# Clipping a gradient by its norm: larger transfers, another split of the work between two engines, and a smaller first store

## The chip, the cores and the metric

One core of a Trainium2 chip. The metric is device time in microseconds (us) of one execution. Some executions of a kernel come out some per cent longer than the others; a run more than 1.5% above the fastest of its kernel is called slow here. Every profiled execution in this study was in the fast state with a granted clock of 1.00; one timed run was slow (52.76 us, in e8), and verdicts use fast runs alone. A profiled execution has a span (here about 1.8 us shorter than the device time of the same execution, 49.9 against 51.7 for the kernel before), and all positions below are microseconds from the start of that span. Sixteen transfer (DMA) engines move the data. In the packet records here one row of a tile is one packet, the 128 rows of a transfer are shared among the sixteen engines, and each engine reports its part with one small completion packet.

## The reference

```python
batch, dim = 512, 4096                      # grad: 512 x 4096 float32, 8.4 MB
norm  = np.sqrt(np.sum(grad ** 2))
scale = min(1.0, max_norm / (norm + 1e-8))  # max_norm = 1.0
return (grad * scale).astype(np.float32)
```

Nothing can be stored before everything has been loaded, since the scale depends on all elements. The whole gradient fits into on-chip memory as four blocks of 128 rows, so it is read once and written once. With the input here the norm is over ten thousand, and the added 1e-8 is far below one unit in the last place.

## The kernel before

Loads of 2048 columns, each squared partly on ScalarE (ACT) and partly on VectorE (DVE); the last 2048 columns are loaded as 1536 and 512, and the 512 go to DVE alone.

```python
LOAD_COLS = 2048; TAIL_COLS = 512; ACT_SQ = 768; ST_COLS = 2048; ACT_MUL = 896
for b, c0, w in loads:
    nc.sync.dma_start(out=gt[b][:, c0:c0+w], in_=g[b*P:(b+1)*P, c0:c0+w])
    a_w = min(ACT_SQ, w // 2) if w > TAIL_COLS else 0
    if a_w:                                  # ACT: square, row sums into one column of acc
        nc.scalar.activation(out=sq, in_=gt[b][:, c0:c0+a_w], func=Square,
                             accum_out=acc[:, icol:icol+1]); icol += 1
    nc.vector.tensor_tensor_reduce(          # DVE: the other columns
        out=sqd, in0=gt[b][:, c0+a_w:c0+w], in1=gt[b][:, c0+a_w:c0+w],
        op0=mult, op1=add, accum_out=acc[:, icol:icol+1], ...); icol += 1

nc.vector.reduce_sum(out=s, in_=acc, axis=X)
nc.tensor.matmul(tot, ones, s, start=True, stop=True)     # sum over partitions
nc.scalar.activation(out=nrm, in_=tot, func=Sqrt, bias=0.0)
nc.vector.tensor_scalar(out=nrm2, in0=nrm, scalar1=1e-8, op0=add, ...)
nc.vector.reciprocal(out=inv, in_=nrm2)
nc.vector.tensor_scalar(out=scale, in0=inv, scalar1=max_norm, scalar2=1.0, op0=mult, op1=min)

for b in range(4):
    for c0 in (0, 2048):                     # DVE 1152 columns, ACT 896, then one store of both
        nc.vector.tensor_scalar(out=gt[b][:, c0:c0+1152], ..., scalar1=scale, op0=mult)
        nc.scalar.mul(gt[b][:, c0+1152:c0+2048], ..., scale)
        nc.sync.dma_start(out=o[...], in_=gt[b][:, c0:c0+2048])
# ... (pools, constants and the launch are cut)
```

Of the kernel before, what the change touches and what calls it, by code (L numbers as in the profile page):

```python
# [1 line left out]

# [4 lines left out]


@with_exitstack  # L10
def kernel(
    ctx: ExitStack,
    tc: tile.TileContext,
    grad: bass.AP,
    max_norm: bass.AP,
    out: bass.AP,
):
    nc = tc.nc
    fp32 = mybir.dt.float32
    bf16 = mybir.dt.bfloat16  # L20

    g = grad.flatten_outer_dims()
    o = out.flatten_outer_dims()
    R, C = g.shape
    P = nc.NUM_PARTITIONS
    assert R % P == 0, (R, P)
    nrow_blk = R // P

    LOAD_COLS = 2048
    TAIL_COLS = 512  # L30
    ACT_SQ = 768
    ST_COLS = 2048
    ACT_MUL = 896
    assert C % LOAD_COLS == 0 and C % ST_COLS == 0

    loads = []
    for b in range(nrow_blk):
        for j in range(C // LOAD_COLS):
            c0 = j * LOAD_COLS
            w = LOAD_COLS  # L40
            if b == nrow_blk - 1 and j == C // LOAD_COLS - 1 and TAIL_COLS:
                loads.append((b, c0, LOAD_COLS - TAIL_COLS))
                loads.append((b, c0 + LOAD_COLS - TAIL_COLS, TAIL_COLS))
            else:
                loads.append((b, c0, w))

    sbuf = ctx.enter_context(tc.tile_pool(name="gbuf", bufs=1))
    small = ctx.enter_context(tc.tile_pool(name="small", bufs=1))
    scratch = ctx.enter_context(tc.tile_pool(name="scratch", bufs=3))
    psum_pool = ctx.enter_context(tc.tile_pool(name="psum", bufs=2, space=bass.MemoryType.PSUM))  # L50

    gt = [sbuf.tile([P, C], fp32, name=f"g{b}", tag=f"g{b}") for b in range(nrow_blk)]

    n_acc = sum(2 if w > TAIL_COLS else 1 for _, _, w in loads)
    acc = small.tile([P, n_acc], fp32)
    ones = small.tile([P, P], fp32)
    zcol = small.tile([P, 1], fp32)
    dcol = small.tile([P, 1], fp32)
    nc.gpsimd.memset(ones, 1.0)  # L59
    nc.gpsimd.memset(zcol, 0.0)  # L60

    nc.scalar.activation(out=dcol, in_=zcol, func=mybir.ActivationFunctionType.Sqrt)  # L62

    icol = 0
    for b, c0, w in loads:
        nc.sync.dma_start(  # L66
            out=gt[b][:, c0 : c0 + w],
            in_=g[b * P : (b + 1) * P, c0 : c0 + w],
        )
        a_w = min(ACT_SQ, w // 2) if w > TAIL_COLS else 0  # L70
        if a_w:
            sq = scratch.tile([P, a_w], bf16, name="sqa", tag="sqa")
            nc.scalar.activation(  # L73
                out=sq,
                in_=gt[b][:, c0 : c0 + a_w],
                func=mybir.ActivationFunctionType.Square,
                accum_out=acc[:, icol : icol + 1],
            )
            icol += 1
        d_w = w - a_w  # L80
        sqd = scratch.tile([P, d_w], bf16, name="sqd", tag="sqd")
        nc.vector.tensor_tensor_reduce(  # L82
            out=sqd,
            in0=gt[b][:, c0 + a_w : c0 + w],
            in1=gt[b][:, c0 + a_w : c0 + w],
            scale=1.0,
            scalar=0.0,
            op0=mybir.AluOpType.mult,
            op1=mybir.AluOpType.add,
            accum_out=acc[:, icol : icol + 1],  # L90
        )
        icol += 1
    assert icol == n_acc

    s = small.tile([P, 1], fp32)
    nc.vector.reduce_sum(out=s, in_=acc, axis=mybir.AxisListType.X)  # L96

    tot = psum_pool.tile([P, 1], fp32, name="tot", tag="tot")
    nc.tensor.matmul(tot, ones, s, start=True, stop=True)  # L99

    nrm = small.tile([P, 1], fp32)
    nc.scalar.activation(  # L102
        out=nrm, in_=tot, func=mybir.ActivationFunctionType.Sqrt, bias=0.0
    )
    nrm2 = small.tile([P, 1], fp32)
    nc.vector.tensor_scalar(  # L106
        out=nrm2, in0=nrm, scalar1=1e-8, scalar2=None, op0=mybir.AluOpType.add
    )
    inv = small.tile([P, 1], fp32)
    nc.vector.reciprocal(out=inv, in_=nrm2)  # L110
    scale = small.tile([P, 1], fp32)
    nc.vector.tensor_scalar(  # L112
        out=scale,
        in0=inv,
        scalar1=float(max_norm),
        scalar2=1.0,
        op0=mybir.AluOpType.mult,
        op1=mybir.AluOpType.min,
    )

    for b in range(nrow_blk):
        for j in range(C // ST_COLS):
            c0 = j * ST_COLS
            dcols = ST_COLS - ACT_MUL
            nc.vector.tensor_scalar(  # L125
                out=gt[b][:, c0 : c0 + dcols],
                in0=gt[b][:, c0 : c0 + dcols],
                scalar1=scale[:, 0:1],
                scalar2=None,
                op0=mybir.AluOpType.mult,  # L130
            )
            nc.scalar.mul(  # L132
                gt[b][:, c0 + dcols : c0 + ST_COLS],
                gt[b][:, c0 + dcols : c0 + ST_COLS],
                scale[:, 0:1],
            )
            nc.sync.dma_start(
                out=o[b * P : (b + 1) * P, c0 : c0 + ST_COLS],
                in_=gt[b][:, c0 : c0 + ST_COLS],
            )  # L140


# [1 line left out]
_INS = ['grad', 'max_norm']  # L144
_OUTS = [((512, 4096), 'float32')]
#: Inputs that are plain numbers.
_NUMBERS = {'max_norm': 1.0}


# [26 lines left out]
```

## Time and profile before

| | before |
|---|---|
| time, median | 51.41 us in 3 runs at first; 51.44 us in the 15 runs beside the changed kernel |
| span of the profiled execution | 49.92 us |
| last-but-one load piece (1536 columns) landed | 22.97 |
| first store issued / its first packet | 27.55 / 28.40 |
| last packet of the last store ended / its completion landed | 48.57 / 48.93 |

Issues are read in the timeline, the first store's in this line (SPq is the queue of SyncE, which issues all transfers):

```profile
27.55 8.97 SPq L137 DMA_DIRECT2D out_dram<-g  x8
```

Packets and landings are in the trace's packet and semaphore records (a landing is the arrival of the last engine's completion signal, some tenths of a microsecond after the last packet). The views themselves are shown in the prediction. In short: load at full transfer rate, a gap with idle transfer engines, store at full rate.

### The profile page before, as it was taken

The page shows a single profiled execution, that of the slowest core. Times are in us where ns is not written, and L with a number is a line of the kernel's source. Part 1 is how long each engine was busy: PE and PEld are TensorE (multiplying, and loading weights), DVE is VectorE, ACT ScalarE, POOL GpSimd, SP SyncE. Part 2 cuts the span into 40 slices and gives each one's busy share as a digit, 9 for nine tenths or more (in the row PEclk, how much of TensorE's full clock was granted, in tenths as well). Part 3 has the DMA queues.
Part 4 walks back from the last instruction along what each step waited for, and adds up shares of the span by engine and source line. Part 5 has one row for each costly group of instructions (what it writes and reads, how often), then busy time and mean ns, then how long its engine had stood idle before and what let it go on. Part 6 is the DMA issues. An engine that isn't in the chain of part 4 may idle for free.

```text
span 49.9 us, 148 instructions
## 1 busy us (share of the span) xinstructions
PE 0.6 (1%) x2; PEld 0.5 (1%) x2; DVE 18.6 (37%) x30; ACT 16.7 (33%) x27; POOL 0.4 (1%) x6
## 2 busy tenths in 40 slices
PE   0000000000000000000040000000000000000000
PEld 0000000000000000000040000000000000000000
DVE  0000192929192929295929999900000000000000
ACT  4700161515161615155217999992000000000000
POOL 3000000000000000000000000000000000000000
DMA  0699999999999999980000299999999999999970
GB/s 0 118 302 420 427 427 420 427 433 420 433 433 427 420 420 415 402 345 33 0 0 0 105 420 420 420 420 420 420 420 420 420 420 420 420 420 420 420 315 0
DMA packets 2448, 16.78 MB, mean 336 GB/s; under 512 B 272, under 2 KB 272, under 8 KB 528
## 3 DMA queue, kind: packets, MB, share of 16 engines
q1 hardware_dynamic: 2448, 16.78, 82.0%
HBM read 8.39 MB, written 8.39 MB: 336 GB/s over the span
## 4 chain that ended last, share of the span: by engine, by line
DMA 37%; ACT 14%; SPq 7%; DVE 4%; issue 2%; ACTq 2%; PE 1%; DVEq 0%
DMA g<-in_grad_dram 37%; ACT g L132 13%; SPq L66 7%; DVE sqd L82 2%; ACTq L171 2%; PE tot L99 1%; DVE s L96 0%; ACT nrm L102 0%; DVE inv L110 0%; DVE nrm L106 0%; DVE scale L112 0%; DVE acc L82 0%; DVEq L96 0%; DVEq L82 0%
## 5 line engine op out<-in xcount | busy, mean ns | idle before, releaser
L82 DVE CUSTOM_DVE_ANT_0 sqd<-g 128x1280 bf16<-128x1280 f32 (+2 forms) x9 | 12.0, 1344 | 12.6 <-DMA g<-in_grad_dram 12.6
L73 ACT ACTIVATE sqa<-g 128x768 bf16<-128x768 f32 x8 | 6.7, 843 | 14.3 <-DMA g<-in_grad_dram 14.3
L132 ACT ACTIVATE g<-g,scale 128x896 f32<-128x896 f32 x8 | 7.6, 1028 | 0.6 <-DVE scale L112 0.6
L125 DVE TENSOR_SCALAR g<-g,scale 128x1152 f32<-128x1152 f32 x8 | 5.9, 815 | 0.0
L62 ACT ACT_TABLE_LOAD x1 | 1.3, 1283 | 0.7 <-PEq L157 0.7
L73 ACT ACTIVATION_READ_ACCUMULATOR sqa<-g 128x1 f32 x8 | 1.5, 187 | 0.0
L99 PE MATMUL tot<-s,ones 128*128 128x1 f32 x2 | 0.6, 348 | 25.1 <-DVE s L96 25.1
L99 PEld LDWEIGHTS tot<-s,ones 128*128 128x128 f32 x2 | 0.5, 313 | 25.1 <-issue 25.1
L82 DVE DVE_READ_ACCUMULATOR2_ANT acc<- 128x1 f32 x9 | 0.7, 83 | 0.0
L102 ACT ACTIVATE nrm<-tot 128x1 f32<-128x1 f32 x1 | 0.2, 171 | 1.7 <-PE tot L99 1.7
L106 DVE TENSOR_SCALAR nrm<-nrm 128x1 f32<-128x1 f32 x1 | 0.2, 155 | 0.9 <-ACT nrm L102 0.9
L96 DVE TENSOR_REDUCE s<-acc 128x1 f32<-128x17 f32 x1 | 0.2, 172 | 0.1
L59 POOL MEMSET ones<- 128x128 f32 x1 | 0.2, 205 | 0.3 <-POOLq L157 0.3
L62 ACT ACTIVATE dcol<-zcol 128x1 f32<-128x1 f32 x1 | 0.2, 203 | 0.0
L110 DVE RECIPROCAL inv<-nrm 128x1 f32<-128x1 f32 x1 | 0.2, 164 | 0.0
L112 DVE TENSOR_SCALAR scale<-inv 128x1 f32<-128x1 f32 x1 | 0.2, 154 | 0.0
L157 POOL MEMSET const-bfloat16-1.0<- 128x1 bf16 x1 | 0.1, 102 | 0.0
L157 POOL MEMSET const-uint8-127<- 128x1 uint8 x1 | 0.1, 102 | 0.0
L157 POOL MEMSET const-float32-0.0<- 128x1 f32 x1 | 0.1, 99 | 0.2 <-issue 0.2
L60 POOL MEMSET zcol<- 128x1 f32 x1 | 0.1, 99 | 0.0
L157 POOL MEMSET const-float32-1.0<- 128x1 f32 x1 | 0.1, 98 | 0.0
## 6 DMA issues: line engine op xcount, KB each, us to landing
out_dram<-g SPq DMA_DIRECT2D x8, 1024.0 KB, 9.3
g<-in_grad_dram SPq DMA_DIRECT2D x7, 1024.0 KB, 11.4
g<-in_grad_dram SPq DMA_DIRECT2D x1, 768.0 KB, 18.4
g<-in_grad_dram SPq DMA_DIRECT2D x1, 256.0 KB, 17.5
```

Source lines behind the costliest of these rows:

```text
L59: nc.gpsimd.memset(ones, 1.0)
L62: nc.scalar.activation(out=dcol, in_=zcol, func=mybir.ActivationFunctionType.Sqrt)
L66: nc.sync.dma_start(out=gt[b][:, c0 : c0 + w], in_=g[b * P : (b + 1) * P, c0 : c0 + w],)
L73: nc.scalar.activation(out=sq, in_=gt[b][:, c0 : c0 + a_w], func=mybir.ActivationFunctionType.Square, accum_out=acc[:, icol : icol + 1],)
L82: nc.vector.tensor_tensor_reduce(out=sqd, in0=gt[b][:, c0 + a_w : c0 + w], in1=gt[b][:, c0 + a_w : c0 + w], scale=1.0, scalar=0.0, op0=myb ...
L96: nc.vector.reduce_sum(out=s, in_=acc, axis=mybir.AxisListType.X)
L99: nc.tensor.matmul(tot, ones, s, start=True, stop=True)
L102: nc.scalar.activation(out=nrm, in_=tot, func=mybir.ActivationFunctionType.Sqrt, bias=0.0)
L125: nc.vector.tensor_scalar(out=gt[b][:, c0 : c0 + dcols], in0=gt[b][:, c0 : c0 + dcols], scalar1=scale[:, 0:1], scalar2=None, op0=mybir.Alu ...
L132: nc.scalar.mul(gt[b][:, c0 + dcols : c0 + ST_COLS], gt[b][:, c0 + dcols : c0 + ST_COLS], scale[:, 0:1],)
L157: nc = _bacc.Bacc("TRN2", target_bir_lowering=False, num_devices=1)
L171: with _tile.TileContext(nc) as tc:
```

## The change

The intent is to spend less on the transfers themselves (whole rows of 16 KB instead of halves of 8 KB), to shorten the serial part between load and store, and to start the store with a small piece. Which engine multiplies what is changed to match. The change also lowers two buffer counts (scratch 3 to 2, PSUM 2 to 1), which no run tests alone; e1 keeps the old counts and shows the same gap. Core of the diff, with cuts marked:

```diff
+    for b in range(nb - 1):
+        loads.append((b, 0, C, None))                 # three loads of 128 x 4096
+    loads.append((lb, 0, C - PRE - TAIL, None))       # 2048 columns
+    loads.append((lb, C - PRE - TAIL, PRE, "A"))      # 1536
+    loads.append((lb, C - TAIL, TAIL, "D"))           # 512, DVE alone
...
-        a_w = min(ACT_SQ, w // 2) if w > TAIL_COLS else 0
+            a_w = 1152 if eng == "A" else (w * 5 // 8) & ~7
...
-    nc.vector.tensor_scalar(
-        out=nrm2, in0=nrm, scalar1=1e-8, scalar2=None, op0=mybir.AluOpType.add
-    )
-    nc.vector.reciprocal(out=inv, in_=nrm2)
+    nc.vector.reciprocal(out=inv, in_=nrm)
...
-    (eight stores of 2048 columns, each DVE 1152 + ACT 896)
+    stores.append((0, 0, 512, [("D", 0, 512)]))
+    stores.append((0, 512, 1024, [("A", 512, 1024)]))
+    stores.append((0, 1536, C - 1536, [("D", 1536, C - 1536)]))
+    stores.append((1, 0, C, [("A", 0, C)]))
+    stores.append((2, 0, C, [("D", 0, C)]))
+    stores.append((3, 0, C, [("A", 0, C // 2), ("D", C // 2, C // 2)]))
```

More of the change, by code (lines that the diff above doesn't have):

```diff
@@ L7 @@
 from concourse._compat import with_exitstack
+CFG = dict(
+    TAIL_COLS=512,
+    PRE_TAIL=1536,
+    ST_FIRST=1024,
+)
 @with_exitstack
@@ L26 @@
     assert R % P == 0, (R, P)
-    nrow_blk = R // P
-    LOAD_COLS = 2048
-    TAIL_COLS = 512
-    ACT_SQ = 768
-    ST_COLS = 2048
-    ACT_MUL = 896
-    assert C % LOAD_COLS == 0 and C % ST_COLS == 0
-    loads = []
-    for b in range(nrow_blk):
-        for j in range(C // LOAD_COLS):
-            c0 = j * LOAD_COLS
-            w = LOAD_COLS
-            if b == nrow_blk - 1 and j == C // LOAD_COLS - 1 and TAIL_COLS:
-                loads.append((b, c0, LOAD_COLS - TAIL_COLS))
-                loads.append((b, c0 + LOAD_COLS - TAIL_COLS, TAIL_COLS))
-            else:
-                loads.append((b, c0, w))
+    nb = R // P
+    TAIL = CFG["TAIL_COLS"]
+    PRE = CFG["PRE_TAIL"]
+    ST_FIRST = CFG["ST_FIRST"]
     sbuf = ctx.enter_context(tc.tile_pool(name="gbuf", bufs=1))
     small = ctx.enter_context(tc.tile_pool(name="small", bufs=1))
-    scratch = ctx.enter_context(tc.tile_pool(name="scratch", bufs=3))
-    psum_pool = ctx.enter_context(tc.tile_pool(name="psum", bufs=2, space=bass.MemoryType.PSUM))
-    gt = [sbuf.tile([P, C], fp32, name=f"g{b}", tag=f"g{b}") for b in range(nrow_blk)]
-    n_acc = sum(2 if w > TAIL_COLS else 1 for _, _, w in loads)
-    acc = small.tile([P, n_acc], fp32)
+    scratch = ctx.enter_context(tc.tile_pool(name="scratch", bufs=2))
+    psum_pool = ctx.enter_context(tc.tile_pool(name="psum", bufs=1, space=bass.MemoryType.PSUM))
+    gt = [sbuf.tile([P, C], fp32, name=f"g{b}", tag=f"g{b}") for b in range(nb)]
+    acc = small.tile([P, 16], fp32)
     ones = small.tile([P, P], fp32)
+    nc.gpsimd.memset(ones, 1.0)
     zcol = small.tile([P, 1], fp32)
     dcol = small.tile([P, 1], fp32)
-    nc.gpsimd.memset(ones, 1.0)
     nc.gpsimd.memset(zcol, 0.0)
     nc.scalar.activation(out=dcol, in_=zcol, func=mybir.ActivationFunctionType.Sqrt)
+    loads = []
+    for b in range(nb - 1):
+        loads.append((b, 0, C, None))
+    lb = nb - 1
+    loads.append((lb, 0, C - PRE - TAIL, None))
+    loads.append((lb, C - PRE - TAIL, PRE, "A"))
+    loads.append((lb, C - TAIL, TAIL, "D"))
     icol = 0
-    for b, c0, w in loads:
+    for b, c0, w, eng in loads:
         nc.sync.dma_start(
@@ L69 @@
         )
-        a_w = min(ACT_SQ, w // 2) if w > TAIL_COLS else 0
-        if a_w:
+        if eng != "D":
+            a_w = 1152 if eng == "A" else (w * 5 // 8) & ~7
             sq = scratch.tile([P, a_w], bf16, name="sqa", tag="sqa")
@@ L79 @@
             icol += 1
-        d_w = w - a_w
-        sqd = scratch.tile([P, d_w], bf16, name="sqd", tag="sqd")
-        nc.vector.tensor_tensor_reduce(
-            out=sqd,
-            in0=gt[b][:, c0 + a_w : c0 + w],
-            in1=gt[b][:, c0 + a_w : c0 + w],
-            scale=1.0,
-            scalar=0.0,
-            op0=mybir.AluOpType.mult,
-            op1=mybir.AluOpType.add,
-            accum_out=acc[:, icol : icol + 1],
-        )
-        icol += 1
-    assert icol == n_acc
+            d_w = w - a_w
+            sqd = scratch.tile([P, d_w], bf16, name="sqd", tag="sqd")
+            nc.vector.tensor_tensor_reduce(
+                out=sqd,
+                in0=gt[b][:, c0 + a_w : c0 + w],
+                in1=gt[b][:, c0 + a_w : c0 + w],
+                scale=1.0,
+                scalar=0.0,
+                op0=mybir.AluOpType.mult,
+                op1=mybir.AluOpType.add,
+                accum_out=acc[:, icol : icol + 1],
+            )
+            icol += 1
+        else:
+            sqd = scratch.tile([P, w], bf16, name="sqd", tag="sqd")
+            nc.vector.tensor_tensor_reduce(
+                out=sqd,
+                in0=gt[b][:, c0 : c0 + w],
+                in1=gt[b][:, c0 : c0 + w],
+                scale=1.0,
+                scalar=0.0,
+                op0=mybir.AluOpType.mult,
+                op1=mybir.AluOpType.add,
+                accum_out=acc[:, icol : icol + 1],
+            )
+            icol += 1
+    n_used = icol
     s = small.tile([P, 1], fp32)
-    nc.vector.reduce_sum(out=s, in_=acc, axis=mybir.AxisListType.X)
+    nc.vector.reduce_sum(out=s, in_=acc[:, 0:n_used], axis=mybir.AxisListType.X)
     tot = psum_pool.tile([P, 1], fp32, name="tot", tag="tot")
@@ L104 @@
     )
-    nrm2 = small.tile([P, 1], fp32)
-    nc.vector.tensor_scalar(
-        out=nrm2, in0=nrm, scalar1=1e-8, scalar2=None, op0=mybir.AluOpType.add
-    )
     inv = small.tile([P, 1], fp32)
-    nc.vector.reciprocal(out=inv, in_=nrm2)
+    nc.vector.reciprocal(out=inv, in_=nrm)
     scale = small.tile([P, 1], fp32)
@@ L119 @@
     )
-    for b in range(nrow_blk):
-        for j in range(C // ST_COLS):
-            c0 = j * ST_COLS
-            dcols = ST_COLS - ACT_MUL
-            nc.vector.tensor_scalar(
-                out=gt[b][:, c0 : c0 + dcols],
-                in0=gt[b][:, c0 : c0 + dcols],
-                scalar1=scale[:, 0:1],
-                scalar2=None,
-                op0=mybir.AluOpType.mult,
-            )
-            nc.scalar.mul(
-                gt[b][:, c0 + dcols : c0 + ST_COLS],
-                gt[b][:, c0 + dcols : c0 + ST_COLS],
-                scale[:, 0:1],
-            )
-            nc.sync.dma_start(
-                out=o[b * P : (b + 1) * P, c0 : c0 + ST_COLS],
-                in_=gt[b][:, c0 : c0 + ST_COLS],
-            )
+    stores = []
+    stores.append((0, 0, 512, [("D", 0, 512)]))
[4 more added lines that the diff above has]
+    stores.append((3, 0, C, [("A", 0, C // 2), ("D", C // 2, C // 2)]))
+    for b, c0, w, ops in stores:
+        for e, sc0, sw in ops:
+            if e == "D":
+                nc.vector.tensor_scalar(
+                    out=gt[b][:, sc0 : sc0 + sw],
+                    in0=gt[b][:, sc0 : sc0 + sw],
+                    scalar1=scale[:, 0:1],
+                    scalar2=None,
+                    op0=mybir.AluOpType.mult,
+                )
+            else:
+                nc.scalar.mul(
+                    gt[b][:, sc0 : sc0 + sw],
+                    gt[b][:, sc0 : sc0 + sw],
+                    scale[:, 0:1],
+                )
+        nc.sync.dma_start(
+            out=o[b * P : (b + 1) * P, c0 : c0 + w],
+            in_=gt[b][:, c0 : c0 + w],
+        )
 _INS = ['grad', 'max_norm']
```

## The prediction

> **What bounds the kernel now.** I began with the page's forty slices, because one core moving 8.4 MB in and 8.4 MB out is first of all a question of the transfer engines.
>
> ```profile
> DVE  0000192929192929295929999900000000000000
> ACT  4700161515161615155217999992000000000000
> ...
> DMA  0699999999999999980000299999999999999970
> GB/s 0 118 302 420 427 427 420 427 433 420 433 433 427 420 420 415 402 345 33 0 0 0 105 420 420 420 420 420 420 420 420 420 420 420 420 420 420 420 315 0
> ```
>
> A slice is 49.9/40 = 1.25 us. The DMA row is full from slice 2 to 17 (the load), idle from 18 to 21, full from 22 to 37 (the store). DVE and ACT are half idle during the load and finished long before the store ends. So time is startup + load + a gap + store + ending, and the compute engines matter only in the gap. The table of stretches gives the rates.
>
> ```profile
> 6.00:20.00 14.00, 0.00 (x0) 0.00 (x0) 8.92 (x12) 5.62 (x12) 0.00 (x0) 1.00 1.01 426
> ...
> 34.00:48.50 14.50, 0.00 (x0) 0.00 (x0) 0.00 (x0) 0.06 (x1) 0.00 (x0) 1.00 1.00 416
> ```
>
> The last column is GB/s: 426 loading, 416 storing, DMA share 1.00. The gap is in the timeline, whose columns are start, length, engine, line and what it did:
>
> ```profile
> 23.06 0.84 ACT L73 ACTIVATE sqa<-g 128x768 bf16<-128x768 f32 x1 [1.10 <-DMA g<-in_grad_dram]
> 23.11 0.96 DVE L82 CUSTOM_DVE_ANT_0 sqd<-g 128x768 bf16<-128x768 f32 x1 [0.54 <-DMA g<-in_grad_dram]
> 23.99 0.69 DVE L82 CUSTOM_DVE_ANT_0 sqd<-g 128x512 bf16<-128x512 f32 x1
> 24.79 0.17 DVE L96 TENSOR_REDUCE s<-acc 128x1 f32<-128x17 f32 x1
> ...
> 25.70 0.17 ACT L102 ACTIVATE nrm<-tot 128x1 f32<-128x1 f32 x1 [1.71 <-PE tot L99]
> 25.91 0.15 DVE L106 TENSOR_SCALAR nrm<-nrm 128x1 f32<-128x1 f32 x1 [0.94 <-ACT nrm L102]
> 26.10 0.16 DVE L110 RECIPROCAL inv<-nrm 128x1 f32<-128x1 f32 x1
> 26.30 0.15 DVE L112 TENSOR_SCALAR scale<-inv 128x1 f32<-128x1 f32 x1
> 26.48 1.05 ACT L132 ACTIVATE g<-g,scale 128x896 f32<-128x896 f32 x1 [0.61 <-DVE scale L112]
> 26.48 0.82 DVE L125 TENSOR_SCALAR g<-g,scale 128x1152 f32<-128x1152 f32 x1
> ```
>
> The reader is to see a serial chain: the last-but-one load piece (1536 columns) is squared on both engines, then DVE alone squares the last 512, then sum, matmul, root, add, reciprocal, scale, then the first multiply. The first store is issued only when the slower half of its 2048 columns is done, ACT's 1.05 us, at 27.55; its first packet starts 0.85 us later (packet records: 28.40). The 512 columns at 23.99 waited for DVE, not for data: the issue table has the 256 KB piece landing 17.5 us after its issue at 6.06, so at 23.6.
>
> ```profile
> g<-in_grad_dram SPq DMA_DIRECT2D x1, 768.0 KB, 18.4
> g<-in_grad_dram SPq DMA_DIRECT2D x1, 256.0 KB, 17.5
> ```
>
> **What the Trainium skill says.** First, "ScalarE: Activation LUTs", section "What ACT_TABLE_LOAD costs": an ACTIVATE with immediate scale and bias takes 186 ns + 0.833 ns per column, each pointer operand adds about 93 ns, back-to-back ones overlap by about 93 ns. The trace agrees: 896 columns with a pointer scale give 279 + 746 = 1025 ns against a mean of 1028; the 768-column square gives 826 against 843, so I add 17 ns for the accumulating form. Second, "VectorE: DVE Perf Modes", section "The perf-mode tier table": fp32 tensor_scalar runs at 2x, fp32 tensor_tensor at 1x, of 0.96 GHz. The trace agrees: 1152 columns in 815 ns is 600 ns of streaming plus 215 fixed; the squares (1280 in 1492 ns, 768 in 958, 512 in 689) have a slope of 1.04 ns and about 158 fixed. Third, "DMA: Bandwidth & Descriptors", section "Why small descriptors are slow (HBM only)", speaks of a fixed cost for every packet. The packet records here agree: median 309 ns for 8 KB and 84 ns for 2 KB, hence (309 - 84)/6144 = 0.0366 ns a byte and about 9 ns fixed. No run yet shows a 16 KB row.
>
> **The change, part by part.**
>
> Loads become three of 2 MB (rows of 16 KB), one of 1 MB, then 1536 and 512 columns as before. Fewer, later landings harm nothing: ACT's 2560-column square takes 186 + 17 + 2133 = 2.34 us and DVE's 1536 columns 158 + 1600 = 1.76 us, while a 2 MB load takes 2 x 2.5 us. The 1 MB piece should land near 21.0 (the seventh piece did: DVE started on it at 21.07); ACT's 1280 columns then take 1.27 us plus the 0.19 accumulator read, until 22.4, before the 1536 piece comes. If a 16 KB row goes as one packet, an engine (8 rows of each load) has 24 packets fewer: 24 x about 10 ns = 0.24 us.
>
> Tail squares: the 1536 piece is now 1152 on ACT and 384 on DVE. ACT: 23.06 + (203 + 960 - 93 + 186 ns) = 24.32, and after its semaphore the sum could start near 24.4. DVE: the 384 columns occupy it for 0.48 us (the 768 occupied it 23.11 to 23.99, 0.88, less 384 x 1.04 = 0.40), so it is free at 23.59 and the last 512 must wait for its landing at 23.6, starting near 23.7. In before the sum came 0.80 after the start of the 512 (24.79 - 23.99), so now 24.50. Gain 0.29, and the last piece's landing becomes the binding event, with ACT 0.1 behind it.
>
> The add of 1e-8 goes: from its start to that of the reciprocal, 26.10 - 25.91 = 0.19 us, all on the path. The sum over 11 columns instead of 17 is worth only nanoseconds.
>
> First multiply: 512 columns on DVE alone, 215 + 512/1.92 = 482 ns instead of 1.05 us. Gain 0.57, all on the path.
>
> Will the store stay fed afterwards? Take scale as ready at 26.48 - 0.29 - 0.19 = 26.00. Store 1 (512 columns) is issued at 26.50 and its data flow from 27.35; 8 packets of 2 KB per engine take about 0.7, to 28.05. ACT's 1024 columns take 279 + 853 = 1.13 us, so store 2 is issued at 27.15 and can flow from 28.0: no bubble. It lasts 8 x 160 ns = 1.3, to 29.3. DVE's 2560 columns (1.55 us) end at 28.03, data can flow from 28.9. That store lasts 3.1, to 32.4. ACT's 4096 columns (3.69 us, less the overlap) end at 30.75, data from 31.6: margin 0.8. DVE's 4096 (2.35 us) end at 30.4. ACT's last 2048 end by 32.7, ten microseconds before they are due. So the store is bandwidth-bound from first byte to last, and the very uneven sharing (whole blocks to one engine) is hidden. Packets per engine fall from 64 to 48: 16 x 10 = 0.16 us.
>
> Sum: 0.29 + 0.19 + 0.57 = 1.05 us from the gap, which I trust, and up to 0.24 + 0.16 = 0.40 from packets, of which I count 0.30 because a 16 KB row may be cut in two. 51.41 - 1.05 - 0.30 = 50.06, about 2.6% less.
>
> **The rivals.**
>
> A: no packet gain, rows of 16 KB are cut into 8 KB packets, or the store rate is limited by something else. For it: stores ran at 416 against 426 for loads of the same packet size, so the write side has a limit of its own. Against it: the 2 KB records show a fixed part. It would give 51.41 - 1.05 = 50.36, just on the 2% line; this is what the chances hinge on.
>
> B: a landing takes the place of the DVE wait. The last load piece's sixteen parts landed between 22.55 and 23.61 in the trace, so one slow transfer engine now sets the start of the last 512 columns. In a run where that engine is worse, or the larger packets widen the spread, the 0.29 is lost: about 50.35 with the packet gain, 50.65 without. The reverse holds too: where the spread is narrower, ACT's 1152 columns bind instead, at 24.4.
>
> C: a bubble in the store. Store 2 has a margin of only 0.05 us, and the first small transfer is over in 0.7 us. If issuing takes longer when two come close together (issue instructions in this trace last from 343 to 1210 ns, the long ones with a deep queue), the engines stand idle for some tenths: 50.3 to 50.4. The first two store issues took 347 and 343 ns, which speaks against it.
>
> D: the change gives nothing because the loads, fewer and larger, start worse: the first packets of the load took 400 to 1300 ns instead of 309, and with 16 KB packets that ramp could cost more. It would add perhaps 0.3 us, to 50.4.
>
> **Range and chances.** Run to run the kernel before varies by 0.14 us, so the range comes from the mechanism. All small effects going well (packets 0.40, landings narrower) give 49.8; A together with half of C or B gives 50.45. I take 49.75 to 50.45. The 2% line lies at 50.38. It takes A plus one more loss, or B and D together, to end above it: I put 0.82 on faster by over 2%, 0.17 on within, 0.01 on slower, since nothing here adds work to the path.
>
> **What would show it.** In the profile after: the first store issue about 1.05 us earlier, near 26.5 (or 26.3 with faster loads); its multiply at 0.48 us; no add between root and reciprocal; the last 512-column square released by the transfer, not by DVE; the idle DMA slices falling from four to about three; load rate above 430 and fewer than 2000 packets if the packet gain is real, more than 2000 packets if A holds. A DMA slice below 9 between the first store and the end would show C. I am wrong if the first store is not issued earlier, or if it is and the end does not follow.

## The result, and the profile after

| | before | after |
|---|---|---|
| time, median (range) | 51.44 us (51.23 to 51.73, 15 runs) | 50.32 us (50.17 to 50.47, 12 runs) |
| ratio of the fast runs | | 0.978 (95%: 0.9761 to 0.9799) |
| span | 49.92 | 48.69 |
| 1536 piece landed | 22.97 | 22.84 |
| first store issued / first packet | 27.55 / 28.40 | 26.40 / 27.24 |
| last packet ended / landed | 48.57 / 48.93 | 47.24 / 47.62 |

A ratio is the mean time of one kernel's fast runs over the mean of the other's of the same rounds, so it is not quite the ratio of the medians quoted beside it. The change made the kernel faster, by 1.12 us in the medians. The line of 2% is passed by little: the interval ends at 0.9799, and when the same kernel was timed again (e9: 0.9783, 0.9765 to 0.9801) the verdict at that line was unclear.

The slices of the changed kernel (1.22 us each), to be read against the same four rows in the prediction:

```profile
DVE  0000000850086007762919999700000000000000
ACT  4800000891089107995817999970000000000000
...
DMA  0969999999999999994000699999999999999950
GB/s 0 202 202 390 431 431 431 431 431 431 431 431 431 424 384 429 406 397 182 0 0 0 244 399 449 446 401 431 431 431 431 431 431 431 431 431 431 431 215 0
```

Load and store are still full, DVE and ACT still have room. The 431 GB/s here against 420 before is not a faster transfer. A packet counts in the slice in which it starts, and in both kernels a steady slice holds 512 KB, two packets of 16 KB or four of 8 KB on each engine; only the slice is shorter, 1.22 us instead of 1.25. The rates must be taken from landings and from first to last packet, as below. The fall-off at both ends of the load is still there. The gap, in the timeline of the changed kernel:

```profile
22.92 1.16 ACT L71 ACTIVATE sqa<-g 128x1152 bf16<-128x1152 f32 x1 [0.53 <-DMA g<-in_grad_dram]
22.97 0.56 DVE L80 CUSTOM_DVE_ANT_0 sqd<-g 128x384 bf16<-128x384 f32 x1 [0.93 <-DMA g<-in_grad_dram]
23.59 0.69 DVE L93 CUSTOM_DVE_ANT_0 sqd<-g 128x512 bf16<-128x512 f32 x1
24.39 0.16 DVE L107 TENSOR_REDUCE s<-acc 128x1 f32<-128x11 f32 x1
...
25.30 0.17 ACT L113 ACTIVATE nrm<-tot 128x1 f32<-128x1 f32 x1 [1.12 <-PE tot L110]
25.50 0.16 DVE L117 RECIPROCAL inv<-nrm 128x1 f32<-128x1 f32 x1 [0.94 <-ACT nrm L113]
25.70 0.15 DVE L119 TENSOR_SCALAR scale<-inv 128x1 f32<-128x1 f32 x1
25.88 6.64 ACT L147 ACTIVATE g<-g,scale 128x1024 f32<-128x1024 f32 x3 [0.42 <-DVE scale L119]
25.89 5.41 DVE L139 TENSOR_SCALAR g<-g,scale 128x512 f32<-128x512 f32 x4
26.40 6.66 SPq L152 DMA_DIRECT2D out_dram<-g  x6
```

The last line is the queue of stores: the first is issued at 26.40, 0.70 us after the scale's start (25.70), where before it was 27.55 - 26.30 = 1.25. The reciprocal follows the root directly. From DVE's start on the 1536 piece to the sum it is 24.39 - 22.97 = 1.42 us, before 24.79 - 23.11 = 1.68.

Where the time came from, end to end in these two profiles:

| stretch | before | after | gain |
|---|---|---|---|
| start to landing of the 1536 piece | 22.97 | 22.84 | 0.13 |
| from there to the first store's issue | 4.58 | 3.56 | 1.02 |
| issue to first packet | 0.85 | 0.84 | 0.01 |
| first to last packet of the store | 20.17 | 20.00 | 0.17 |
| last packet to end of span | 1.35 | 1.45 | -0.10 |
| span | 49.92 | 48.69 | 1.23 |

Two rows need experiments. Is 0.13 at the load an effect of the larger rows or of one execution? And why did the ending grow?

### The profile page after: what moved, and what is told of

It is laid out like the page before. It is cut to its first block, busy times and chain, and to the rows that moved or that the text cites. A ratio compares the mean times of both kernels' runs of the same rounds, so it can differ in the third digit from the quotient of the medians.

```text
span 48.7 us, 114 instructions
## 1 busy us (share of the span) xinstructions
PE 0.6 (1%) x2; PEld 0.5 (1%) x2; DVE 13.4 (28%) x19; ACT 18.2 (37%) x16; POOL 0.4 (1%) x6
## 2 busy tenths in 40 slices
DMA packets 1728, 16.78 MB, mean 345 GB/s; under 512 B 192, under 2 KB 192, under 8 KB 704
## 3 DMA queue, kind: packets, MB, share of 16 engines
q1 hardware_dynamic: 1728, 16.78, 83.5%
## 4 chain that ended last, share of the span: by engine, by line
DMA 41%; ACTq 7%; ACT 7%; SPq 4%; DVE 4%; issue 1%; PE 1%; DVEq 0%
DMA g<-in_grad_dram 41%; ACTq L186 7%; ACT g L147 6%; SPq L64 4%; DVE sqd L93 1%; PE tot L110 1%; DVE sqd L80 1%; ACT nrm L113 0%; DVE inv L117 0%; DVE s L107 0%; DVE scale L119 0%; DVEq L107 0%; DVEq L80 0%; DVE acc L80 0%; DVE acc L93 0%
## 5 line engine op out<-in xcount | busy, mean ns | idle before, releaser
L71 ACT ACTIVATE sqa<-g 128x2560 bf16<-128x2560 f32 (+2 forms) x5 | 9.4, 1889 | 12.1 <-DMA g<-in_grad_dram 12.0
L80 DVE CUSTOM_DVE_ANT_0 sqd<-g 128x1536 bf16<-128x1536 f32 (+2 forms) x5 | 6.8, 1358 | 16.7 <-DMA g<-in_grad_dram 16.7
L147 ACT ACTIVATE g<-g,scale 128x1024 f32<-128x1024 f32 (+2 forms) x3 | 6.6, 2277 | 0.4 <-DVE scale L119 0.4
L139 DVE TENSOR_SCALAR g<-g,scale 128x512 f32<-128x512 f32 (+3 forms) x4 | 5.4, 1416 | 0.0
L71 ACT ACTIVATION_READ_ACCUMULATOR sqa<-g 128x1 f32 x5 | 0.9, 186 | 0.0
L93 DVE CUSTOM_DVE_ANT_0 sqd<-g 128x512 bf16<-128x512 f32 x1 | 0.7, 693 | 0.0
```

The source lines that it names most:

```text
L71: nc.scalar.activation(out=sq, in_=gt[b][:, c0 : c0 + a_w], func=mybir.ActivationFunctionType.Square, accum_out=acc[:, icol : icol + 1],)
L80: nc.vector.tensor_tensor_reduce(out=sqd, in0=gt[b][:, c0 + a_w : c0 + w], in1=gt[b][:, c0 + a_w : c0 + w], scale=1.0, scalar=0.0, op0=myb ...
L93: nc.vector.tensor_tensor_reduce(out=sqd, in0=gt[b][:, c0 : c0 + w], in1=gt[b][:, c0 : c0 + w], scale=1.0, scalar=0.0, op0=mybir.AluOpType ...
L139: nc.vector.tensor_scalar(out=gt[b][:, sc0 : sc0 + sw], in0=gt[b][:, sc0 : sc0 + sw], scalar1=scale[:, 0:1], scalar2=None, op0=mybir.AluOp ...
L147: nc.scalar.mul(gt[b][:, sc0 : sc0 + sw], gt[b][:, sc0 : sc0 + sw], scale[:, 0:1],)
```

## The experiments

Twelve kernels ran, each timed in five rounds. Differences against the changed kernel are taken from the two ratios to the kernel before, times 51.4 us; the changed kernel's own ratio was 0.978 in the first set of runs and 0.9783 again in e9. The intervals of the ratios are 0.1 to 0.2 us wide to each side, so the traces carry the finer readings.

**e1: the gap alone.** The kernel before, with the three edits between load and store only:

```diff
-        a_w = min(ACT_SQ, w // 2) if w > TAIL_COLS else 0
+        a_w = (1152 if w == 1536 else min(ACT_SQ, w // 2)) if w > TAIL_COLS else 0
...
-    (the add of 1e-8)
+    if b == 0 and j == 0:   # DVE 512, stored; then ACT 1024 and DVE 512, stored as 1536
```

> The kernel before with the three edits of the gap alone: the 1536 piece split 1152/384, no add of 1e-8, and the first 2048 columns stored as 512 (DVE alone) and then 1536. Loads and all other stores keep rows of 8 KB. Theory (the gain is the shorter chain between load and store; larger rows give next to nothing): the first store is issued 1.0 us earlier than before, near 26.5, and the time is 50.4 us, within 0.15 of the changed kernel. Rival (packets of 16 KB give 0.4 us of the 1.12): 50.75. Rival (nothing gained in the gap reaches the end): 51.4.

Measured: 50.46 us, ratio 0.9829, so 0.25 us longer than the changed kernel. From the landing of the 1536 piece (22.60) to the first store's issue (26.16) it took 3.56 us, exactly as in the changed kernel. The store took 20.26 us from first to last packet, against 20.00: about the whole difference (the ending was 1.05 us against 1.07). Most of the gain is the shorter gap, as the first theory says; the rival's 0.4 from packets is too much, and the 0.25 that is left lies in the store.

**e2: 8 KB rows in the load again.**

```diff
-        nc.sync.dma_start(out=gt[b][:, c0 : c0 + w], ...)
+        for q0 in range(c0, c0 + w, 2048):
+            nc.sync.dma_start(out=gt[b][:, q0 : min(q0 + 2048, c0 + w)], ...)
```

> The changed kernel with each 16 KB row loaded as two transfers with rows of 8 KB; squares, chain and stores unchanged. Theory (the fixed cost saved per packet is paid back in a slower start: the first 2 MB landed at 8.67 against 8.49 before): first block lands near 8.5, the 1 MB piece still near 20.9, and the time is within 0.1 of the changed kernel, 50.3 to 50.4. Rival (24 packets fewer per engine at 10 ns are a net gain): 0.24 slower, 50.56.

Measured: 49.98 us (49.94 to 50.24), ratio 0.9723: 0.3 us *faster* than the changed kernel, which neither theory had foreseen (the profiled execution was the slowest of its six, 50.24). In the trace the load is neither better nor worse, as the theory said: the 1536 piece lands at 22.83 against 22.84, the last store at 47.57 against 47.62. The difference shows behind that: from the last landing to the end of the span it is 0.88 us here and 1.07 in the changed kernel. This is what e9 to e12 follow up.

**e3: 8 KB rows in the store again.** Each of the three 2 MB stores is issued as two of 1 MB, after the same multiplies.

> The changed kernel with each of the three 2 MB stores issued as two transfers with rows of 8 KB once the whole block is multiplied: 24 packets more per engine. Theory (about 10 ns for every packet): 0.2 to 0.25 us slower, 50.55. Rival (the store rate has its own limit and row length gives nothing): the same, 50.32.

Measured: 50.43 us, ratio 0.9807, 0.14 longer. In the trace the store took 20.29 us against 20.00: 0.29 for 24 packets more per transfer engine, 12 ns each (three completions of 9 ns are in it). The packet records show the same: in the store a packet of 16 KB takes 616 ns in the mean, two of 8 KB 630. So the fixed cost per packet in the store is real. It did not reach the time in full, because the ending was again shorter (0.88 us instead of 1.07).

**e4: the tail split as before.** `a_w = 1152` becomes `a_w = 768`.

> The changed kernel with the 1536 piece split 768/768 again. Theory (DVE's queue of two squares is what starts the sum): DVE free 0.40 us later, the 512-column square starts near 23.85 to 23.9 instead of 23.59, the first store is issued 0.3 to 0.4 later, and the time is 50.62 to 50.72. Rival (the landing of the last piece or the ACT square binds anyway): within 0.1 of the changed kernel.

Measured: 50.53 us, ratio 0.9834, 0.28 longer with an uncertainty of about 0.1. The timeline has DVE's start on the piece and the sum:

```profile
22.78 0.96 DVE L80 CUSTOM_DVE_ANT_0 sqd<-g 128x768 bf16<-128x768 f32 x1 [0.93 <-DMA g<-in_grad_dram]
24.47 0.17 DVE L107 TENSOR_REDUCE s<-acc 128x1 f32<-128x11 f32 x1
```

They are 1.69 us apart, as before the change (1.68) and 0.27 more than in the changed kernel. It is less than the 0.40 that DVE saves, so something else had begun to bind. That is e7's question.

**e5: the first store as before.** The first three entries of `stores` become one of 2048 columns (DVE 1152, ACT 896) and one of 2048 (DVE).

> The changed kernel with its first store as before: 2048 columns, 1152 on DVE and 896 on ACT, then the other 2048 of that block on DVE. Theory (the first multiply lies wholly on the path): the first store is issued 0.53 us later (1026 ns against about 490) and the time is 0.45 to 0.55 longer, 50.8, the two packets per row fewer giving back at most 0.1. Rival (the small first store opens a bubble, so the early start is partly lost): less than 0.3 longer.

Measured: 50.80 us in the median, 0.48 longer; the ratio 0.9915 says 0.7: one of its eight runs took 51.33, and the kernel before ran 0.12 faster in these rounds. The timeline has the scale and the first store's issue:

```profile
25.45 0.15 DVE L119 TENSOR_SCALAR scale<-inv 128x1 f32<-128x1 f32 x1
26.70 0.35 SPq L151 DMA_DIRECT2D out_dram<-g  x1
```

They are 1.25 us apart, as before the change, against 0.70 in the changed kernel: 0.55. There is no bubble that gives part of it back: the store took 20.00 us with the small first pieces and 19.93 without, for 8 packets fewer per engine.

**e6: the add put back.**

> The changed kernel with the add of 1e-8 put back between root and reciprocal. Theory: 0.19 to 0.20 us later at the first store and at the end, 50.52. Rival (the end is set by something other than the chain): the same.

Measured: 50.48 us, ratio 0.9834, 0.16 longer by the medians and 0.28 by the ratios. In its timeline the add starts at 25.38 and the reciprocal at 25.57, so the trace puts 0.19 us on it.

**e7: more of the tail on ACT.** `a_w = 1152` becomes `a_w = 1280`.

> The changed kernel with the 1536 piece split 1280/256 instead of 1152/384. Theory (three things end within 0.15 us of each other: DVE, the landing of the last piece at 23.45, and ACT's square): DVE gains at most 0.1 because the last 512 columns then wait for their landing, and ACT's square ends 0.107 later at about 24.28, so the sum starts within 0.08 of where it did and the time is the same within 0.1. Rival (DVE alone binds): 0.13 faster.

Measured: 50.36 us (50.16 to 50.76), ratio 0.9808: no gain, and by the ratio 0.14 longer, though the intervals overlap. The timeline of e7 shows why DVE's shorter square buys nothing:

```profile
22.76 0.43 DVE L80 CUSTOM_DVE_ANT_0 sqd<-g 128x256 bf16<-128x256 f32 x1 [0.92 <-DMA g<-in_grad_dram]
23.11 0.08 DVE L80 DVE_READ_ACCUMULATOR2_ANT acc<- 128x1 f32 x1
23.38 0.69 DVE L93 CUSTOM_DVE_ANT_0 sqd<-g 128x512 bf16<-128x512 f32 x1 [0.19 <-DMA g<-in_grad_dram]
23.89 0.19 ACT L71 ACTIVATION_READ_ACCUMULATOR sqa<-g 128x1 f32 x1
24.00 0.08 DVE L93 DVE_READ_ACCUMULATOR2_ANT acc<- 128x1 f32 x1
24.18 0.16 DVE L107 TENSOR_REDUCE s<-acc 128x1 f32<-128x11 f32 x1
```

DVE now stands idle for 0.19 us before the last 512 columns, and the bracket names the transfer. ACT's accumulator read ends at 24.08, as DVE's does. From DVE's start on the piece to the sum it is 24.18 - 22.76 = 1.42, the changed kernel's value. In the changed kernel itself the 512 columns landed at 23.45 and their square began 0.14 later; its other DVE square began 0.13 after its landing (22.84 to 22.97). So there too it was the landing that started it, and the changed split already sits where DVE, ACT and the last landing meet.

**e8: a fine-grained start.** The first block is loaded in eight pieces of 512 columns.

> The changed kernel with the first block loaded in eight pieces of 512 columns (rows of 2 KB), the other loads unchanged: does the start of the load depend on the size of the first packets? Theory (large first packets start slowly): the first block lands earlier than 8.67 although it costs 40 more packets per engine than e2's fixed cost of 10 ns would make 0.5 later; so the net is between 0.1 faster and 0.3 slower. Rival (the start costs the same whatever the packet size, only the fixed cost counts): 0.5 slower at the first landing and at the end, 50.8. Issue time of about 0.45 us for each of eight 256 KB pieces, which take about 0.7 to move, should not bind.

Measured: 52.26 us, ratio 1.0153, 1.9 longer than the changed kernel. Both theories missed. I had counted 40 packets more per engine; it is 64 instead of 8, so 56. In the trace's completion records the eight pieces landed 0.93 us apart in the mean (3.83 for the first, 10.37 for the eighth, each by its last engine), so 117 ns for a 2 KB packet with its share of the completion, where I had reckoned with 84 or so. A better start from small packets is refuted: the second block was squared from 15.26 instead of 13.59.

**e9 to e12: the ending.** The queue that issues the transfers also waits for all their completions at the end. Completions use eight semaphores in turn, and the final waits stand in a fixed order, two semaphores to most of them. The semaphore of the last store is the one that matters, and what stands behind its wait is still worked off. These are the final waits with the last landing, from the trace's records (not a view of the profile); e4, e6 and e7 have 12 transfers and end as the changed kernel does:

```
kernel  transfers  waits behind the last store's   last landing to end of span, us
e11     19         5                               48.68 to 49.81   1.13
e8      19         5                               49.29 to 50.41   1.12
e5      11         5                               47.87 to 48.99   1.12
after   12         4                               47.62 to 48.69   1.07
e9      12         4                               47.65 to 48.72   1.07
e1      18         4                               47.61 to 48.66   1.05
before  17         3                               48.93 to 49.92   0.99
e3      15         1                               47.64 to 48.53   0.88
e2      15         1                               47.57 to 48.45   0.88
e10     16         0                               48.08 to 48.90   0.82
e12     16         0                               47.85 to 48.67   0.82
```

e10 and e11 were made to move only this, with loads that nobody reads:

```diff
+    for k in range(4):      # e11: range(7)
+        dum = small.tile([16, 512], fp32, ...)
+        nc.sync.dma_start(out=dum, in_=g[16 * k : 16 * k + 16, 0:512])
```

> The changed kernel itself, unaltered, so that the next three runs can be compared with it on the same chip in the same rounds. Both theories: 0.978 of the kernel before, about 50.3 us; span end 1.05 to 1.1 us after the landing of the last store.

Measured: 50.26 us, ratio 0.9783, as the first time.

> The changed kernel with four extra loads of 32 KB into tiles that nothing reads, issued after the last real load; they land while the transfer engines are idle. They do nothing but move the last store from the fourth of the eight completion semaphores, which are used in turn, to the eighth. Theory (after the last landing the queue's engine still works off the waits that stand behind that store's own, about 61 ns each; in the changed kernel five, here none or one): the part from the last landing to the end of the span falls from 1.07 to about 0.82, and the time is 0.2 to 0.25 shorter than e9. Rival (e2 was faster because its 1 MB loads start better): no change, or some 0.1 longer for the extra transfers.

> The same with seven extra loads, which puts the last store on the third semaphore, the one waited for first, so that all the other waits come after its landing. Theory: last landing to end of span 1.13, time 0.06 longer than e9 and 0.31 longer than e10. Rival (more or earlier transfers in themselves change the time): e11 differs from e9 in the same direction as e10, and by more.

Measured: e10 50.85 us (0.9912), e11 51.67 us (1.0071). As a timing experiment both failed, for they added work to the path. The extra loads were issued behind the last real piece, yet that piece landed at 23.92 in e10 and 24.51 in e11, against 23.47 in e9. In e10's timeline the last square waits for it:

```profile
24.06 0.69 DVE L93 CUSTOM_DVE_ANT_0 sqd<-g 128x512 bf16<-128x512 f32 x1 [0.68 <-DMA g<-in_grad_dram]
```

Why a later transfer delays an earlier one here is open; the 2 KB packets of the load took 100 ns in the mean in e10 and 121 in e11, against 84 in the changed kernel. As an experiment on the ending they succeeded: the rows of the table go as expected (0.82 and 1.13 predicted, 0.82 and 1.13 measured; I had said five waits behind the changed kernel's last store, and it is four). The waits of the queue itself show the order. First e10, then e11; the columns are who waited for what, us in total, times, longest:

```profile
SPq L190 <- DMA out_dram<-g: 14.3, 3, 4.9
```

```profile
SPq L190 <- DMA out_dram<-g: 14.5, 1, 14.5
```

e10 waits for its stores in order of issue, last one last. e11 waits first for the last one, 14.5 us at one wait, and has all the other waits still to go.

> The best that the runs so far point to: the changed kernel with its blocks loaded in 1 MB pieces (e2) and one extra load of 32 KB, so that the last store falls on the eighth semaphore. Theory (the waits after the last landing are worth 0.06 each, the size of the loads next to nothing): as e10 within 0.1, 50.05. Rival (1 MB loads give 0.3 by themselves): 0.3 shorter than e10.

Measured: 50.26 us, ratio 0.9796, no better than the changed kernel and 0.3 to 0.4 slower than e2. Its ending is 0.82 us, but one extra load was enough to land the last piece at 23.70 instead of e2's 23.43. So the best kernel of the study is e2, at 49.98 us: 2.8% faster than before, and faster than the changed kernel.

## Why the prediction was right

**The gap.** Predicted 1.05 us, measured 1.02. By its steps: tail squares 0.29 predicted, 0.26 between the two timelines and 0.27 by undoing it (e4); the add 0.19, measured 0.20 between the timelines, which includes the few nanoseconds of the shorter sum, and 0.19 in e6; the first multiply 0.57, measured 0.55 in both ways. e1 has these edits alone and shows the same 3.56 us from landing to issue.

**The landing that becomes binding** (rival B's starting point). Right, and shown by e7. Its cost was in the 0.29 already (0.40 less on DVE, 0.11 of waiting for the landing). The rest of the gain was not lost, because the last piece landed 0.62 us behind the 1536 piece, where before it was 0.63: the spread that rival B feared did not come.

**The store stays fed** (against rival C). Right: 20.00 us from first to last packet, and e5 shows no bubble bought back.

**Packets in the store.** Predicted up to 0.16, measured 0.17, and e3 gives 12 ns per packet where I had used 10. Rival A, in its form "16 KB rows are cut", is refuted by the page: `DMA packets 1728` with rows of 16 KB in the packet records. The number that spoke for A, 416 GB/s against 426, was misread: both stretches count whole packets by their start. Landings of 1 MB pieces came 2.48 us apart in the load before and 2.50 in the store. (A small slip beside it: in the DMA row before, slice 22 is only two tenths full; the store fills the slices 23 to 37.)

**Packets in the load.** This is the term that was mis-sized: up to 0.24 us, of which nothing came. The saving per packet was there, but the start of the load took it back, which is rival D's mechanism. The completion records show both. The table has means over the sixteen engines, from four executions with 8 KB rows (before, e1, e2, e12) and nine with 16 KB rows (changed kernel, e3 to e7, e9 to e11):

| | 8 KB rows | 16 KB rows |
|---|---|---|
| first 2 MB landed | 7.91 to 8.00 | 8.07 to 8.17 |
| from there to the landing of the 1 MB piece | 12.42 to 12.43 | 12.26 to 12.27 |
| 1 MB piece landed | 20.33 to 20.43 | 20.33 to 20.44 |

Once the load runs, 16 data packets and 2 completions fewer per engine save 0.16 us, 10 ns per data packet, as I had used. But the first 2 MB come about 0.17 later instead of 0.08 sooner: the first sixteen packets of the load took 1.30 to 1.49 us each in the mean with 16 KB rows (0.61 later on) and 0.66 to 0.76 with 8 KB rows (0.31 later on). Why they are so slow is not shown. The gain of 0.13 at the load, in the table of the result, is therefore the difference of two executions: the 1536 piece landed at 22.60 to 22.97 with 8 KB rows and at 22.59 to 22.88 with 16 KB rows. In the time, e1 leaves no room for a gain here (its 0.25 is about the store's), and e2 has no loss from giving it up.

**The ending.** Not in the prediction at all. The changed kernel has 12 transfers instead of 17, which happens to put one more wait behind the last store's: 0.08 us from landing to end.

Together: 1.02 + 0.17 + 0 - 0.08 = 1.11 us, against 1.12 measured. The forecast of 50.06 was 0.26 too low, for the most part for the two reasons above: 0.30 counted for packets of which 0.17 came, and the ending. That the 2% were still passed is in part luck: the prediction put the case without any gain from packets at 50.36, just on the line, and 0.17 of the packet gain came, of which 0.08 was lost again in the ending.

**The signs.** Of what was to show it, the first store's issue (26.40), its multiply (0.49 us), the missing add, three idle slices, fewer than 2000 packets and no slice below 9 inside the store all came. A load rate above 430 did not: the table of stretches gives 426 from 6 to 20 us in both kernels, and between the landings of the first 2 MB and of the 1 MB piece it is 422 before and 428 after.

**What stays open.** e2 is 0.3 us faster than the changed kernel. 0.19 of that is the ending, shown in its trace. The other 0.1 is no larger than the intervals; one profile of each shows no cause for it. Why the extra loads of e10 to e12 delay the piece ahead of them is open as well.

## What to carry to other kernels

Where two bandwidth-bound phases are separated by a serial chain, each 0.1 us off the chain was about 0.1 us off the time here (e4, e5, e6), and a small first piece restarts the transfers sooner. By the prediction's reckoning it should be just large enough to hide the next one; only 512 columns and 2048 were tried. Balance the last piece so that both engines and its own landing end together, and stop there; e7 shows that more gives nothing. Before blaming a transfer's size for a few tenths, look behind the last landing: how many waits the queue still has to work off depends on how many transfers there were, and it moved by 0.3 us here between e10 and e11. And take a rate from landings, not from slices or short stretches: those count whole packets and can differ by some per cent for the same transfer.

## What the Trainium skill lacked or had wrong

- "DMA: Bandwidth & Descriptors", section "Why small descriptors are slow (HBM only)": it names a fixed cost per packet, and joining packets is called worthwhile only at 256 B or less. At rows of 8 KB, doubling the row still saved 12 ns per packet in the store (e3: 0.29 us for 24 packets) and 10 ns in the running load (0.16 us for 16).
- That a load starts more slowly with larger rows I found on no page: the first sixteen packets took 1.30 to 1.49 us in the mean with rows of 16 KB against 0.61 later on, and the first 2 MB landed about 0.17 us later than with rows of 8 KB.
- I found the cost of the final waits on no page: 0.06 us for each wait that stands behind the last store's, 0.82 us with none and 1.13 with five.
- Nor does a page that I read say that small loads issued behind a load can delay it: with four of 32 KB the last piece landed at 23.92, with seven at 24.51, against 23.47 without.
- "ScalarE: Activation LUTs", section "What ACT_TABLE_LOAD costs": the formula held (4096 columns with a pointer scale: 3.69 us worked out from it, 3695 ns in the trace), but it lacks the read of the accumulator that follows a summing ACTIVATE, 186 ns each here.
